# Two of four weight block sums of an MLP's first product: from VectorE to accumulating DMAs

## The chip, the cores and the metric

One core of one Trainium2 chip. The metric is the device time of one execution in microseconds (us); the runs shown are three, and their median is taken.

## The reference

One layer of an encoder on x of 512 tokens by 2048 features, all in float32: `h = x + conformer_conv(rms_norm(x))`, then `h = h + mlp(rms_norm(h))`, then a last RMS norm. Only the MLP matters here:

```python
def sq_relu_mlp(h, w_up, w_down):          # w_up [2048, 8192], w_down [8192, 2048]
    return jnp.square(jax.nn.relu(h @ w_up)) @ w_down
```

## The kernel before

**Matmuls.** A float32 product is made of float32r products: each operand is split into a high part (a cast) and a low part (what the cast left), and a product is three matmuls, high by high, high by low and low by high (`mm3`, lines 199 to 202). Weights are the stationary operand, 128 by 128; activations stream as 512 or 256 columns.

**Pieces.** All weights are fetched as a list of pieces of 512 KB (`pieces`, `fetch`, line 128), in the order in which TensorE (PE) uses them. A piece lands in a `wr` buffer by a DMA on SyncE's queue (SP), ScalarE (ACT) casts it into `wh` (the high part), VectorE (DVE) subtracts it into `wl` (the low part). `wr`, `wh` and `wl` have 3 buffers each. `prep(n)` (line 188) emits the fetches two pieces further than the splits.

**The first product (up).** It is computed with 7 block products in place of 8 (a scheme of Strassen and Winograd over 2 by 2 blocks). 32 units of 256 columns of `w_up`, four pieces to a unit. An up piece holds four blocks for two values of k (`wupb`, `BLOCKS` at line 105). Three block products use blocks 1 to 3 as they are (`OF_RAW`, line 825), four use sums of blocks (`OF_SUM`). `split_blocks` (line 169) makes both for a piece: ACT casts blocks 1 to 3 (line 178), DVE adds block 0 to blocks 1 and 2 (line 179: sums 0 and 1), then adds block 2 to sum 0 (line 182: sum 2) and block 3 to sum 2 (line 183: sum 3), takes the low part of the blocks (line 184); ACT casts the four sums (line 185) and DVE takes their low part (line 186). The sums lie in the tile `ws`, one buffer. A piece needs two `wh` and two `wl` buffers, one for the blocks and one for the sums, out of the three of each. On PE (function `up`, line 902) a piece is 18 matmuls with the blocks and then 24 with the sums, all of 256 columns.

**The second product (down).** Pieces of `wdn` of 256 rows by 512 columns; 24 matmuls of 512 columns each (`group`, line 785). Its sums are added to `h` by DVE (line 964).

**Order.** `jobs` (line 116) lists the work: up of units 0, 1 and 2, down of units 0 and 1, up of 3 and 4, down of 2 and 3, and so on, up of 29, 30 and 31, down of the last four. So up pieces come in runs: one of 12, then 13 of 8, then one of 12, with 16 down pieces between two of them. The order on PE is that of the program; on the other engines and the queues a scheduler orders the instructions of this part of the program, and each engine then keeps its order. The waits for buffers come from the tile framework.

**After a unit.** The block products are combined on DVE (lines 935 to 938, tile `c`, tag `W`), one operand having been copied by ACT into `q1` (line 934); relu and the RMS scale `r2` (line 940), the square (ACT, line 943) and the split into `z` (lines 950 and 951) follow. `r2` is made once: the column sums of `Q2` (tag `Q2`) are taken in unit 0 (`ffn_sum`, line 892), a power is taken on GpSimd (POOL, line 248, `rr_ffn`), and `ffn_scale` (line 897) writes `r2`. The tag `Q2` is used again at the end, for `Q3`.

Of the kernel before, what the change touches and what calls it, by code (L numbers as in the profile page):

```python
# [8 lines left out]
F32 = mybir.dt.float32  # L9
F32R = mybir.dt.float32r  # L10
AF = mybir.ActivationFunctionType
ALU = mybir.AluOpType
PSUM = bass.MemoryType.PSUM

P = 128
T = 512
# [11 lines left out]
HT = T // 2  # L28
EDGE = HT + 16

WBUFS = 3


POOL_TAPS = [5, 5, 6, 5] * 3 + [6, 5, 9]
# [15 lines left out]
N_UNITS = DFF // UNIT  # L50
# [4 lines left out]
def conformer_layer(ctx: ExitStack, tc: tile.TileContext, xT, vecs, wdw, w1, w2, wupb, wdn, outT):  # L55
    nc = tc.nc

    const = ctx.enter_context(tc.tile_pool(name="const", bufs=1))
    acts = ctx.enter_context(tc.tile_pool(name="acts", bufs=1))
    wpool = ctx.enter_context(tc.tile_pool(name="wpool", bufs=WBUFS))  # L60
    pp = ctx.enter_context(tc.tile_pool(name="pp", bufs=1, space=PSUM))
# [25 lines left out]
    def col(base, k):  # L87
        return vec[:, base + k : base + k + 1]


    pieces = []
# [10 lines left out]
        for k in range(0, NK, 2):  # L102
            wide(w2, k * P, g * 512)

    BLOCKS = [P, 2, 4, P]

    def up_pieces(u):
        for p in range(4):
            pieces.append((wupb[u, p], BLOCKS))

    def down_pieces(units):
        for g in range(4):
# [9 lines left out]
    for kind, what in jobs:  # L122
        (up_pieces if kind == "up" else down_pieces)(what)

    raws, prepped = {}, {}
    state = {"raw": 0, "prep": 0}

    def fetch(upto):
        while state["raw"] < min(upto, len(pieces)):
            i = state["raw"]  # L130
            src, shape = pieces[i]
            r = wtile(i, "wr", F32)
            if i < n_p1:
                for s in range(2):
                    nc.sync.dma_start(out=r[:, s], in_=src[:, s])
            elif shape is BLOCKS:
                nc.sync.dma_start(out=r.rearrange("p a b c -> p (a b c)"), in_=src)
            else:
                nc.sync.dma_start(out=r, in_=src)
            raws[i] = r  # L140
            state["raw"] += 1

    def home(i, tag):

        if i == n_p1 and tag != "wr":
            return ph1, tag, 1
        if (i < n_p1 and i % 4 == 3) or i == n_p1 + 4:
            return ph1, tag + "4", 1
        return wpool, tag, WBUFS

    def wtile(i, tag, dtype, shape=None):
        pool, tag, bufs = home(i, tag)
        return pool.tile(shape or pieces[i][1], dtype, tag=tag, name=f"{tag}{i}", bufs=bufs)
# [15 lines left out]
    def split_blocks(i):  # L169

        r = raws.pop(i)
        s = wpool.tile(BLOCKS, F32, tag="ws", name=f"ws{i}", bufs=1)
        hr, hs = (wpool.tile([P, 2, n, P], F32R, tag="wh", name=f"wh{i}_{n}", bufs=WBUFS) for n in (3, 4))
        lr, ls = (wpool.tile([P, 2, n, P], F32R, tag="wl", name=f"wl{i}_{n}", bufs=WBUFS) for n in (3, 4))
        prepped[i] = (hr, lr), (hs, ls)
        nc.scalar.copy(out=hr, in_=r[:, :, 1:4])  # L178
        nc.vector.tensor_tensor(
            out=s[:, :, 0:2], in0=r[:, :, 1:3], in1=r[:, :, 0:1].to_broadcast([P, 2, 2, P]), op=ALU.add  # L180
        )
        nc.vector.tensor_add(out=s[:, :, 2], in0=s[:, :, 0], in1=r[:, :, 2])
        nc.vector.tensor_add(out=s[:, :, 3], in0=s[:, :, 2], in1=r[:, :, 3])  # L183
        nc.vector.tensor_tensor(out=lr, in0=r[:, :, 1:4], in1=hr.bitcast(F32), op=ALU.subtract)
        nc.scalar.copy(out=hs, in_=s)  # L185
        nc.vector.tensor_tensor(out=ls, in0=s, in1=hs.bitcast(F32), op=ALU.subtract)  # L186

    def prep(upto):
        fetch(upto + 2)
        while state["prep"] < min(upto, len(pieces)):  # L190
            i = state["prep"]
            state["prep"] += 1
            if pieces[i][1] is BLOCKS:
                split_blocks(i)
# [4 lines left out]
    def mm3(out, wh, wl, xh, xl, start, stop, **kw):  # L199
        nc.tensor.matmul(out, lhsT=wh, rhs=xh, start=start, stop=False, **kw)  # L200
        nc.tensor.matmul(out, lhsT=wh, rhs=xl, start=False, stop=False, **kw)  # L201
        nc.tensor.matmul(out, lhsT=wl, rhs=xh, start=False, stop=stop, **kw)  # L202
# [3 lines left out]
    def bank(tag, name):  # L206
        return pp.tile([P, T], F32, tag=tag, name=name, bufs=banks_of[tag])
# [13 lines left out]
    def spread(dg, out, start=True):  # L221

        nc.tensor.matmul(
            out, lhsT=ones, rhs=dg.rearrange("p a b -> p (a b)"), start=start, stop=True, skip_group_check=True
        )
        return out
# [100 lines left out]
    with tc.manual_schedule(engines=ordered):  # L327
        added = 0
        for k in range(NK):
            ah[k], al[k] = split_scaled(k, x_of(k), col(C_GMIX, k))  # L330
            i, kk = divmod(k, 4)
            if i == 0 or kk % 2 == 0:
# [4 lines left out]
                    out=lo[:, :, part], in0=r, in1=hi[:, :, part].bitcast(F32), op=ALU.subtract  # L337
# [40 lines left out]
    box = {}  # L378
# [163 lines left out]
    for j in range(NK - 1):  # L542
# [16 lines left out]
        if j == NK - 3:  # L559
            box["dgw"] = ph1.tile([P, PE_TAPS, P], F32, tag="xn", name="dgw", bufs=1)  # L560
            for i in range(PE_TAPS):
                c = CW - 1 - i
# [5 lines left out]
    halves = (slice(0, HT), slice(HT, T))  # L568
    banks_a = pw1(last, 0, EDGE, more=True)
    fetch(n_p1 + 5)  # L570
    state["prep"] = n_p1 + 5
    split_hi(n_p1)
# [270 lines left out]
    def place(kt, b):  # L843
        o = pair_operand(kt)
        nc.scalar.copy(out=o[:, :, 0], in_=b[:, 0:7])
        nc.vector.tensor_tensor(out=o[:, :, 1], in0=b[:, 0:7], in1=o[:, :, 0].bitcast(F32), op=ALU.subtract)
        assert len(T4_OF) == kt
        T4_OF.append(o)

    hT = []  # L850
    Q2 = None
    for g in range(4):
# [7 lines left out]
        if g == 0:  # L860
            ph2 = ctx.enter_context(tc.tile_pool(name="ph2", bufs=2, reuse_waits="tile"))
            for i in range(4):
                t = ph2.tile([P, 4, T], F32, tag=f"h{i}", name=f"h{i}", bufs=1)
                nc.sync.dma_start(out=t, in_=xT[i * 4 * P : (i + 1) * 4 * P].rearrange("(k p) t -> p k t", p=P))
                hT.append(t)
            Q2 = ph2.tile([P, T], F32, tag="Q2", name="Q2", bufs=1)
        for m in range(4):
            k = 4 * g + m
            h = hT[g][:, m, :]
            nc.vector.scalar_tensor_tensor(  # L870
                out=h, in0=banks[m], scalar=col(C_BPW2, k), in1=h, op0=ALU.add, op1=ALU.add
            )
            if m % 2 == 0:
# [3 lines left out]
                out=blocks[:, at : at + 2].rearrange("p a b -> p (a b)"), in_=h, func=AF.Copy, scale=col(C_GFFN, k)  # L877
# [7 lines left out]
            if m % 2:  # L885
                form(k // 2, blocks)
                blocks_of[k // 2] = blocks
                if k // 2 < 3 or g == 3:
                    place(k // 2, blocks)
    r2 = const.tile([P, T], F32, name="r2")  # L890

    def ffn_sum():
        b = bank("x", "cs_ffn")
        colsum(b, 0, [Q2], 0, 4, True, True)
        box["dg"] = rms_scale(b, "ffn", ph2)

    def ffn_scale():
        nc.scalar.copy(out=r2, in_=spread(box["dg"], bank("x", "sp_ffn")))

    z_of = {}  # L900

    def up(u):

        n = ng["n"]
        ng["n"] += 1
        banks = [bank("mm" if n % 2 == 0 else "xxxy"[m], f"u{u}_{m}") for m in range(4)]
        i0 = pi["i"]
        pi["i"] += 4
        for p in range(4):
            prep(i0 + p + 2)  # L910
            for (wh, wl), of in zip(prepped.pop(i0 + p), (OF_RAW, OF_SUM)):
                for kk in range(2):
                    kt = 2 * p + kk
                    for b, (x, q, half) in enumerate(of):
                        out = banks[q][:, half * HT : half * HT + HT]
                        xh, xl = T4_OF[kt][:, x, 0], T4_OF[kt][:, x, 1]
                        first = kt == 0 and (of is OF_RAW or (q, half) == (2, 1))
                        mm3(out, wh[:, kk, b], wl[:, kk, b], xh, xl, first, kt == 7, skip_group_check=True)
                if u == 0 and p == 2 and of is OF_RAW:
                    ffn_sum()  # L920
        if u == 0:
            ffn_scale()

        def two(b):
            return b.rearrange("p (a t) -> p a t", a=2)


        c = ph2.tile([P, 6, HT], F32, tag="W", name=f"c{u}", bufs=1)
        q1 = ph2.tile([P, HT], F32, tag="q1", name=f"q1_{u}", bufs=1)

        def bc(a):
            return a[:, None, :].to_broadcast([P, 2, HT])

        nc.scalar.copy(out=q1, in_=banks[0][:, 0:HT])
        nc.vector.tensor_tensor(out=c[:, 2:6:2], in0=two(banks[1]), in1=bc(q1), op=ALU.add)
        nc.vector.tensor_tensor(out=c[:, 3:6:2], in0=two(banks[2]), in1=bc(c[:, 4]), op=ALU.add)
        nc.vector.tensor_tensor(out=c[:, 0:2], in0=two(banks[3]), in1=bc(c[:, 5]), op=ALU.subtract)
        nc.vector.tensor_sub(out=c[:, 3], in0=c[:, 3], in1=banks[3][:, HT:T])
        t = c[:, 0:4].rearrange("p (m a) t -> p m (a t)", m=2)
        nc.vector.scalar_tensor_tensor(  # L940
            out=t, in0=t, scalar=0.0, in1=r2[:, None, :].to_broadcast([P, 2, T]), op0=ALU.max, op1=ALU.mult
        )
        nc.scalar.activation(out=t, in_=t, func=AF.Square)
        if u == N_UNITS - 1:

            zh, zl = slots[0][:, 0:2], slots[0][:, 2:4]
        else:
            z = ph2.tile([P, 2, 2, T], F32R, tag="z", name=f"z{u}", bufs=3)
            zh, zl = z[:, 0], z[:, 1]
        nc.scalar.copy(out=zh, in_=t)  # L950
        nc.vector.tensor_sub(out=zl, in0=t, in1=zh.bitcast(F32))
        z_of[u] = [(zh[:, m], zl[:, m]) for m in range(2)]
# [21 lines left out]
    for g in range(3):  # L974
        banks = group(kc, zh, zl)
        for m in range(4):
            k = 4 * g + m
# [124 lines left out]
```

## Time and profile before

| | |
|---|---|
| median of 3 runs | 1964.34 us (1962.2 to 1964.91) |
| the profiled execution | 1961.89 us |
| its span, first to last instruction | 1959.8 us |
| busy share of the span | PE 98%, DVE 72%, ACT 38%, POOL 20% |
| mean granted clock of PE | 0.994 of full speed |

The rows of a profile say how long each engine was busy, what an engine waited for before it started an instruction (its releaser), and when each instruction started. "PE" is the matmuls; "PEld" the weight loads, which overlap them; a "q" behind an engine's name is its instruction queue, which issues DMAs. Matmuls are pipelined, so the time between two starts, not the duration of one, says how fast PE goes.

### The profile page before, as it was taken

The page shows a single profiled execution, that of the slowest core. Times are in us where ns is not written, and L with a number is a line of the kernel's source. Part 1 is how long each engine was busy: PE and PEld are TensorE (multiplying, and loading weights), DVE is VectorE, ACT ScalarE, POOL GpSimd, SP SyncE. Part 2 cuts the span into 40 slices and gives each one's busy share as a digit, 9 for nine tenths or more (in the row PEclk, how much of TensorE's full clock was granted, in tenths as well). Part 3 has the DMA queues.
Part 4 walks back from the last instruction along what each step waited for, and adds up shares of the span by engine and source line. Part 5 has one row for each costly group of instructions (what it writes and reads, how often), then busy time and mean ns, then how long its engine had stood idle before and what let it go on. Part 6 is the DMA issues. An engine that isn't in the chain of part 4 may idle for free.

```text
span 1959.8 us, 27630 instructions
## 1 busy us (share of the span) xinstructions
PE 1916.5 (98%) x11192; PEld 1697.3 (87%) x11192; DVE 1408.2 (72%) x1918; ACT 735.6 (38%) x903; POOL 386.5 (20%) x266
## 2 busy tenths in 40 slices
PE   8899999989999999999999999999999999999997
PEld 5688888878888898989989899898989989898987
DVE  7999999985468676767667676776767667675844
ACT  5533444553344332423324242332423333242443
POOL 6778899851111000000000000000000000000000
PEclk9999999999999999999999999999999999999999
DMA  7233333125322323333233332323323233333333
GB/s 221 76 97 97 97 97 98 55 72 172 98 86 80 108 87 108 108 91 114 86 112 94 96 112 92 109 87 108 108 86 117 82 113 90 105 108 88 111 99 101
DMA packets 138782, 199.23 MB, mean 102 GB/s; under 512 B 7328, under 2 KB 77216, under 8 KB 138656
## 3 DMA queue, kind: packets, MB, share of 16 engines
q1 hardware_dynamic: 138512, 197.42, 32.9%
q8 instruction: 87, 1.43, 0.3%
q14 instruction: 39, 0.32, 0.1%
q10 hardware_dynamic: 144, 0.07, 0.0%
HBM read 193.27 MB, written 4.19 MB: 101 GB/s over the span
## 4 chain that ended last, share of the span: by engine, by line
issue 69%; PE 24%; DVE 4%; DMA 1%; ACT 1%; SPq 0%; POOL 0%; POOLq 0%; DVEq 0%
PE g L201 3%; PE g L202 3%; PE g L200 3%; PE pa L202 3%; PE pa L201 3%; PE pg L200 3%; PE pg L202 3%; PE pa L200 3%; PE pg L201 3%; DVE slot L295 1%; DMA wr<-w 1%; DVE acc L432 0%; DVE slot L647 0%; DVE wl L167 0%; DMA x<-xT 0%
## 5 line engine op out<-in xcount | busy, mean ns | idle before, releaser
L162 ACT CAST wh<-wr 128x1024 fp32r<-128x1024 f32 x219 | 229.5, 1049 | 470.7 <-PE g L201 315.1
L200 PE MATMUL g<-z,wh 128*128 128x512 f32 (+1 forms) x1016 | 390.6, 384 | 0.0
L201 PE MATMUL g<-z,wh 128*128 128x512 f32 (+1 forms) x1016 | 390.3, 384 | 0.0
L202 PE MATMUL g<-z,wl 128*128 128x512 f32 (+1 forms) x1016 | 390.1, 384 | 0.0
L167 DVE TENSOR_TENSOR wl<-wr,wh 128x1024 fp32r<-128x1024 f32 x159 | 200.5, 1262 | 213.3 <-ACT wh L162 213.1
L202 PE MATMUL u<-slot,wl 128*128 128x256 f32 x1120 | 319.6, 285 | 5.6 <-DVE wl L186 3.7
L200 PE MATMUL u<-slot,wh 128*128 128x256 f32 x1120 | 317.6, 284 | 0.1
L201 PE MATMUL u<-slot,wh 128*128 128x256 f32 x1120 | 317.4, 283 | 0.0
L186 DVE TENSOR_TENSOR wl<-ws,wh 128x1024 fp32r<-128x1024 f32 x128 | 156.8, 1225 | 187.9 <-ACT wh L185 187.0
L248 POOL TENSOR_TENSOR rr_fin<-ms_fin,mhalf 128x2 f32<-128x2 f32 x2 | 1.4, 696 | 1341.3 <-DVE ms_fin L246 1341.3
L185 ACT CAST wh<-ws 128x1024 fp32r<-128x1024 f32 x128 | 134.1, 1048 | 294.7 <-DVE ws L183 138.3
L432 DVE SCALAR_TENSOR_TENSOR acc<-u,wd,acc 128x512 f32<-128x512 f32 (+1 forms) x362 | 237.4, 729 | 0.2
L202 PEld LDWEIGHTS u<-slot,wl 128*128 128x128 f32 x1120 | 215.3, 192 | 9.7 <-DVE wl L186 7.8
L202 PEld LDWEIGHTS g<-z,wl 128*128 128x128 f32 x1016 | 190.9, 188 | 37.8
L200 PEld LDWEIGHTS g<-z,wh 128*128 128x128 f32 x1016 | 190.9, 188 | 37.6
L201 PEld LDWEIGHTS g<-z,wh 128*128 128x128 f32 x1016 | 190.9, 188 | 37.1
L200 PEld LDWEIGHTS u<-slot,wh 128*128 128x128 f32 x1120 | 215.4, 192 | 0.4 <-ACT wh L185 0.3
L201 PEld LDWEIGHTS u<-slot,wh 128*128 128x128 f32 x1120 | 215.4, 192 | 0.0
L202 PE MATMUL u<-T,wl 128*128 128x256 f32 x672 | 190.7, 284 | 1.9 <-DVE wl L186 1.8
L200 PE MATMUL u<-T,wh 128*128 128x256 f32 x672 | 190.7, 284 | 1.0 <-ACT wh L185 1.0
L201 PE MATMUL u<-T,wh 128*128 128x256 f32 x672 | 190.1, 283 | 0.0
L178 ACT CAST wh<-wr 128x768 fp32r<-128x768 f32 x128 | 106.8, 834 | 214.2 <-PE g L201 122.7
(207 smaller groups left out, 3484.0 us busy)
## 6 DMA issues: line engine op xcount, KB each, us to landing
wr<-wupb SPq DMA_DIRECT2D x128, 512.0 KB, 3.6
wr<-wdn SPq DMA_DIRECT2D x128, 512.0 KB, 3.7
wr<-w SPq DMA_DIRECT2D x120, 256.0 KB, 3.3
wr<-w SPq DMA_DIRECT2D x32, 512.0 KB, 3.7
h<-xT SPq DMA_DIRECT2D x4, 1024.0 KB, 10.8
outT<-h SPq DMA_DIRECT2D x14, 256.0 KB, 2.9
x<-xT SPq DMA_DIRECT2D x6, 512.0 KB, 6.0
wr<-w SPq DMA_DIRECT2D x16, 128.0 KB, 5.3
```

The source lines that it names most:

```text
L162: nc.scalar.copy(out=prepped[i][0], in_=r)
L167: eng.tensor_tensor(out=lo, in0=r, in1=hi.bitcast(F32), op=ALU.subtract)
L178: nc.scalar.copy(out=hr, in_=r[:, :, 1:4])
L185: nc.scalar.copy(out=hs, in_=s)
L186: nc.vector.tensor_tensor(out=ls, in0=s, in1=hs.bitcast(F32), op=ALU.subtract)
L200: nc.tensor.matmul(out, lhsT=wh, rhs=xh, start=start, stop=False, **kw)
L201: nc.tensor.matmul(out, lhsT=wh, rhs=xl, start=False, stop=False, **kw)
L202: nc.tensor.matmul(out, lhsT=wl, rhs=xh, start=False, stop=stop, **kw)
L248: nc.gpsimd.tensor_tensor(out=r, in0=ms, in1=mhalf[:, 0:n], op=ALU.pow)
L295: nc.vector.scalar_tensor_tensor(out=lo, in0=src, scalar=g, in1=hi.bitcast(F32), op0=ALU.mult, op1=ALU.subtract)
L432: nc.vector.scalar_tensor_tensor(out=acc if c < end - 1 else vt, in0=u[:, c : c + n], scalar=wd[:, j, c : c + 1], in1=src, op0=ALU.mult, o ...
```

## The change

The weights for up are laid out by the host with the block index ahead of k, so that the tiles are `[P, block, 2, P]`. An up piece's `wr` tile holds blocks 1 to 3 only (384 KB in place of 512 KB). `ws` has two buffers, and is allocated and partly filled when the piece is fetched: one more DMA on SP writes blocks 1 and 2 into its places 0 and 1 (256 KB), and a DMA issued by POOL adds block 0, read from DRAM once for each of the two places, onto both (256 KB). The addition on line 179 is left out. To make room, `r2` moves into the buffer of `Q2`, and `q1` into place 0 of `c`.

```diff
--- before.py
+++ after.py
@@ -29,6 +29,7 @@
 EDGE = HT + 16
 
 WBUFS = 3
+WSBUFS = 2
 
 
 POOL_TAPS = [5, 5, 6, 5] * 3 + [6, 5, 9]
@@ -102,11 +103,11 @@
         for k in range(0, NK, 2):
             wide(w2, k * P, g * 512)
 
-    BLOCKS = [P, 2, 4, P]
+    BLOCKS = [P, 4, 2, P]
 
     def up_pieces(u):
         for p in range(4):
-            pieces.append((wupb[u, p], BLOCKS))
+            pieces.append((wupb[u, p].rearrange("p (b k c) -> p b k c", b=4, k=2), BLOCKS))
 
     def down_pieces(units):
         for g in range(4):
@@ -122,19 +123,30 @@
     for kind, what in jobs:
         (up_pieces if kind == "up" else down_pieces)(what)
 
-    raws, prepped = {}, {}
+    raws, prepped, sums_of = {}, {}, {}
     state = {"raw": 0, "prep": 0}
 
     def fetch(upto):
         while state["raw"] < min(upto, len(pieces)):
             i = state["raw"]
             src, shape = pieces[i]
-            r = wtile(i, "wr", F32)
+            if shape is BLOCKS:
+                r = wtile(i, "wr", F32, [P, 3, 2, P])
+            else:
+                r = wtile(i, "wr", F32)
             if i < n_p1:
                 for s in range(2):
                     nc.sync.dma_start(out=r[:, s], in_=src[:, s])
             elif shape is BLOCKS:
-                nc.sync.dma_start(out=r.rearrange("p a b c -> p (a b c)"), in_=src)
+                nc.sync.dma_start(out=r, in_=src[:, 1:4])
+
+                s = sums_of[i] = wpool.tile([P, 4, 2, P], F32, tag="ws", name=f"ws{i}", bufs=WSBUFS)
+                nc.sync.dma_start(out=s[:, 0:2], in_=src[:, 1:3])
+                nc.gpsimd.dma_start(
+                    out=s[:, 0:2].rearrange("p b k c -> p b (k c)"),
+                    in_=src[:, 0:1].rearrange("p b k c -> p b (k c)").to_broadcast([P, 2, 2 * P]),
+                    accum_op=ALU.add,
+                )
             else:
                 nc.sync.dma_start(out=r, in_=src)
             raws[i] = r
@@ -171,17 +183,14 @@
 
 
         r = raws.pop(i)
-        s = wpool.tile(BLOCKS, F32, tag="ws", name=f"ws{i}", bufs=1)
-        hr, hs = (wpool.tile([P, 2, n, P], F32R, tag="wh", name=f"wh{i}_{n}", bufs=WBUFS) for n in (3, 4))
-        lr, ls = (wpool.tile([P, 2, n, P], F32R, tag="wl", name=f"wl{i}_{n}", bufs=WBUFS) for n in (3, 4))
+        s = sums_of.pop(i)
+        hr, hs = (wpool.tile([P, n, 2, P], F32R, tag="wh", name=f"wh{i}_{n}", bufs=WBUFS) for n in (3, 4))
+        lr, ls = (wpool.tile([P, n, 2, P], F32R, tag="wl", name=f"wl{i}_{n}", bufs=WBUFS) for n in (3, 4))
         prepped[i] = (hr, lr), (hs, ls)
-        nc.scalar.copy(out=hr, in_=r[:, :, 1:4])
-        nc.vector.tensor_tensor(
-            out=s[:, :, 0:2], in0=r[:, :, 1:3], in1=r[:, :, 0:1].to_broadcast([P, 2, 2, P]), op=ALU.add
-        )
-        nc.vector.tensor_add(out=s[:, :, 2], in0=s[:, :, 0], in1=r[:, :, 2])
-        nc.vector.tensor_add(out=s[:, :, 3], in0=s[:, :, 2], in1=r[:, :, 3])
-        nc.vector.tensor_tensor(out=lr, in0=r[:, :, 1:4], in1=hr.bitcast(F32), op=ALU.subtract)
+        nc.scalar.copy(out=hr, in_=r)
+        nc.vector.tensor_add(out=s[:, 2], in0=s[:, 0], in1=r[:, 1])
+        nc.vector.tensor_add(out=s[:, 3], in0=s[:, 2], in1=r[:, 2])
+        nc.vector.tensor_tensor(out=lr, in0=r, in1=hr.bitcast(F32), op=ALU.subtract)
         nc.scalar.copy(out=hs, in_=s)
         nc.vector.tensor_tensor(out=ls, in0=s, in1=hs.bitcast(F32), op=ALU.subtract)
 
@@ -887,14 +896,13 @@
                 blocks_of[k // 2] = blocks
                 if k // 2 < 3 or g == 3:
                     place(k // 2, blocks)
-    r2 = const.tile([P, T], F32, name="r2")
-
     def ffn_sum():
         b = bank("x", "cs_ffn")
         colsum(b, 0, [Q2], 0, 4, True, True)
         box["dg"] = rms_scale(b, "ffn", ph2)
 
     def ffn_scale():
+        r2 = box["r2"] = ph2.tile([P, T], F32, tag="Q2", name="r2", bufs=1)
         nc.scalar.copy(out=r2, in_=spread(box["dg"], bank("x", "sp_ffn")))
 
     z_of = {}
@@ -915,7 +923,7 @@
                         out = banks[q][:, half * HT : half * HT + HT]
                         xh, xl = T4_OF[kt][:, x, 0], T4_OF[kt][:, x, 1]
                         first = kt == 0 and (of is OF_RAW or (q, half) == (2, 1))
-                        mm3(out, wh[:, kk, b], wl[:, kk, b], xh, xl, first, kt == 7, skip_group_check=True)
+                        mm3(out, wh[:, b, kk], wl[:, b, kk], xh, xl, first, kt == 7, skip_group_check=True)
                 if u == 0 and p == 2 and of is OF_RAW:
                     ffn_sum()
         if u == 0:
@@ -926,7 +934,8 @@
 
 
         c = ph2.tile([P, 6, HT], F32, tag="W", name=f"c{u}", bufs=1)
-        q1 = ph2.tile([P, HT], F32, tag="q1", name=f"q1_{u}", bufs=1)
+
+        q1 = c[:, 0]
 
         def bc(a):
             return a[:, None, :].to_broadcast([P, 2, HT])
@@ -938,7 +947,7 @@
         nc.vector.tensor_sub(out=c[:, 3], in0=c[:, 3], in1=banks[3][:, HT:T])
         t = c[:, 0:4].rearrange("p (m a) t -> p m (a t)", m=2)
         nc.vector.scalar_tensor_tensor(
-            out=t, in0=t, scalar=0.0, in1=r2[:, None, :].to_broadcast([P, 2, T]), op0=ALU.max, op1=ALU.mult
+            out=t, in0=t, scalar=0.0, in1=box["r2"][:, None, :].to_broadcast([P, 2, T]), op0=ALU.max, op1=ALU.mult
         )
         nc.scalar.activation(out=t, in_=t, func=AF.Square)
         if u == N_UNITS - 1:
@@ -1064,8 +1073,8 @@
     def blocks(w):
 
         w = w.reshape(4, 2, 2, P, N_UNITS, 2, P)
-        w = np.stack([w[:, :, 1, :, :, 0], w[:, :, 0, :, :, 0], w[:, :, 1, :, :, 1], w[:, :, 0, :, :, 1]], axis=4)
-        return np.ascontiguousarray(w.transpose(3, 0, 2, 1, 4, 5)).reshape(N_UNITS, 4, P, 8 * P)
+        w = np.stack([w[:, :, 1, :, :, 0], w[:, :, 0, :, :, 0], w[:, :, 1, :, :, 1], w[:, :, 0, :, :, 1]], axis=3)
+        return np.ascontiguousarray(w.transpose(4, 0, 2, 3, 1, 5)).reshape(N_UNITS, 4, P, 8 * P)
 
     arrays = {
         "xT": np.ascontiguousarray(a["x"][0].T),
```

## Rows read from the trace of the kernel before

**Rows 1.** The page's first part: busy time, share of the span, instructions.

```profile
span 1959.8 us, 27630 instructions
PE 1916.5 (98%) x11192; PEld 1697.3 (87%) x11192; DVE 1408.2 (72%) x1918; ACT 735.6 (38%) x903; POOL 386.5 (20%) x266
```

**Rows 2.** Windows: stretch, length, busy time (instructions) by engine, PE clock, DMA share, GB/s.

```profile
600.00:640.00 40.00, 37.20 (x294) 35.49 (x294) 32.73 (x47) 15.30 (x20) 1.93 (x1) 1.00 0.30 91
...
800.00:900.00 100.00, 99.99 (x662) 92.28 (x662) 70.91 (x96) 35.60 (x39) 0.00 (x0) 1.00 0.31 96
1300.00:1400.00 100.00, 99.98 (x662) 92.27 (x662) 70.28 (x95) 34.57 (x38) 0.00 (x0) 1.00 0.32 99
...
1800.00:1850.00 50.00, 48.20 (x393) 47.18 (x392) 39.81 (x57) 21.00 (x24) 0.00 (x0) 1.00 0.33 95
```

**Rows 3.** Waits of PE in the up pieces: us in total, times, longest.

```profile
PE u L202 <- DVE wl L186: 5.5, 9, 0.9
...
PE u L202 <- DVE wl L184: 1.7, 1, 1.7
...
PE u L200 <- ACT wh L185: 1.0, 2, 0.5
```

**Rows 4.** Timeline of PE around 1204 us: start, duration, what.

```profile
1200.05 0.39 PE L200 MATMUL g<-z,wh 128*128 128x512 f32 x1
1200.27 0.39 PE L201 MATMUL g<-z,wh 128*128 128x512 f32 x1
...
1204.12 0.28 PE L200 MATMUL u<-T,wh 128*128 128x256 f32 x1
1204.24 0.28 PE L201 MATMUL u<-T,wh 128*128 128x256 f32 x1
...
1209.16 0.28 PE L200 MATMUL u<-T,wh 128*128 128x256 f32 x1
```

**Rows 5.** Timeline of ACT in that run of eight up pieces.

```profile
1206.40 1.05 ACT L185 CAST wh<-ws 128x1024 fp32r<-128x1024 f32 x1 [1.46 <-PE u L201]
...
1222.37 1.05 ACT L185 CAST wh<-ws 128x1024 fp32r<-128x1024 f32 x1 [0.76 <-DVE ws L183]
...
1241.96 0.37 ACT L934 COPY q<-u 128x256 f32<-128x256 f32 x1 [0.31 <-PE u L202]
```

**Rows 6.** Timeline of DVE in that run of eight up pieces.

```profile
1207.48 1.23 DVE L186 TENSOR_TENSOR wl<-ws,wh 128x1024 fp32r<-128x1024 f32 x1 [1.51 <-ACT wh L185]
...
1220.51 0.96 DVE L184 TENSOR_TENSOR wl<-wr,wh 128x768 fp32r<-128x768 f32 x1 [0.88 <-ACT wh L178]
1221.38 0.42 DVE L182 TENSOR_TENSOR ws<-ws,wr 128x256 f32<-128x256 f32 x1
...
1223.45 1.22 DVE L186 TENSOR_TENSOR wl<-ws,wh 128x1024 fp32r<-128x1024 f32 x1 [1.19 <-ACT wh L185]
...
1233.21 1.22 DVE L951 TENSOR_TENSOR z<-c,z 128x1024 fp32r<-128x1024 f32 x1
```

**Rows 7.** Groups by line: count, busy us, mean ns of one, idle before, releaser.

```profile
L179 DVE TENSOR_TENSOR ws<-wr 128x512 f32<-128x512 f32 x128 | 88.1, 688 | 7.1 <-DMA wr<-wupb 5.1
...
L185 ACT CAST wh<-ws 128x1024 fp32r<-128x1024 f32 x128 | 134.1, 1048 | 294.7 <-DVE ws L183 138.3
...
L178 ACT CAST wh<-wr 128x768 fp32r<-128x768 f32 x128 | 106.8, 834 | 214.2 <-PE g L201 122.7
```

**Rows 8.** DMA issues: count, KB each, median us from issue to landing.

```profile
wr<-wupb SPq DMA_DIRECT2D x128, 512.0 KB, 3.6
...
wr<-w SPq DMA_DIRECT2D x120, 256.0 KB, 3.3
...
outT<-h SPq DMA_DIRECT2D x14, 256.0 KB, 2.9
...
outT<-h SPq DMA_DIRECT2D x4, 128.0 KB, 1.8
```

**Rows 9.** The DMA queue of SP: packets, MB, share of 16 engines.

```profile
q1 hardware_dynamic: 138512, 197.42, 32.9%
```

**Rows 10.** Tile wupb: the issuing of its DMAs on SP's queue, duration min/median/max in ns.

```profile
L137 SPq DMA_DIRECT2D wr<-wupb x128: 327/328/341, 558.2 to 1833.3; - x128
```

## The prediction

> **What bounds the kernel now.** I read the page's busy shares first: PE is busy for 98% of the span, and DVE, which the change relieves, for 72% [rows 1]. A share over the whole span proves little, so I cut it: in stretches inside the MLP PE is busy for 99.98 of 100 us, and DVE for 70 of them [rows 2]. The reader is to see that nothing keeps PE waiting there. The gaps that exist lie in the first and the last run of twelve up pieces: 2.8 us in 40 and 1.8 us in 50 [rows 2]. The waits name their causes: PE waited 5.5 us for the low part of the sums, 1.7 for that of the blocks and 1.0 for the cast of the sums, 8.2 us together [rows 3]. That is all that faster preparation of up weights could win; the 88.1 us of additions on line 179 [rows 7] lie beside a busy PE.
>
> Then I took PE's beat from the timeline: a matmul of 256 columns starts every 0.12 us, a piece of 42 every 5.04 (1204.12 to 1209.16), and one of 512 columns every 0.22 to 0.23 [rows 4]. So an up piece allows 5.04 us for everything its weights need. I call S(k) the start of piece k in the run of eight that begins at 1204.12. PE needs the first low part of the sums 18 matmuls and two more later: at S(k) + 2.16 + 0.24 = S(k) + 2.40.
>
> Last I looked at how early the sums are ready. Piece 1 has its low part at 1207.48 + 1.23 = 1208.71 [rows 6], against a need at 1209.16 + 2.40 = 1211.56: 2.85 us to spare. It can't be much earlier, since ACT began the cast at 1206.40, when PE released the `wh` buffer [rows 5].
>
> **What the change costs, part by part.**
>
> *Removed:* 128 additions of 0.69 us on DVE [rows 7]. Cover: PE. Worth 0 where PE doesn't wait, at most the 8.2 us above.
>
> *Layout:* the blocks' cast now reads one straight stretch. Its 768 elements took 834 ns and the sums' 1024, already straight, 1048 [rows 7]: 0.81 us for 768 by proportion where 0.83 was measured. Nothing to win. `q1` in place 0 of `c` must wait for the last reader of the previous `c`, which started at 1233.21 [rows 6] and ran 1.22; `q1` is written at 1241.96 [rows 5]: 7.5 us to spare, so 0. `r2` and `Q3` take over `Q2`'s buffer a group or more after its last reader: 0. The power for the RMS scale shares POOL's queue with the new DMAs in unit 0 and could stand behind one that waits: once, 0 to about 3 us; I take 0.
>
> *SP's queue:* a DMA keeps it 0.33 us [rows 10], two per up piece 0.66 of 5.04. More important, the new DMA of piece k waits until line 186 has freed `ws` of piece k-2, and the blocks of piece k+1 are queued behind it. For piece 4 that is 1208.71. Landing takes 3.6 [rows 8], the cast 0.83 [rows 7] and line 184 0.96 [rows 6]: ready by about 1214.1, where PE starts piece 4 at 1204.12 + 4 x 5.04 = 1224.28. Cost 0, and if PE stalls, the need moves too.
>
> *Bytes:* a piece moves 384 + 256 + 256 = 896 KB in place of 512. The SP queue's packets fill 32.9% of the engines [rows 9], 0.31 to 0.33 in the MLP [rows 2]; times 1.75 that is 0.58 in the up runs. Not a bound, but the landings may lengthen.
>
> *The new chain.* This carries the sum. Sums 0 and 1 no longer come from a 0.69 us instruction on data that landed long ago, but from two DMAs in a row, and the first can't start before the buffer is free. With two buffers a loop closes every two pieces: `ws` freed by line 186 of piece k-2; copy of 256 KB; accumulation, x; lines 182, 183, cast, line 186 of piece k. The copy: 3.3 us (256 KB on this queue; bounds 2.9 for the output's 256 KB, 3.6 for 512 KB [rows 8]). The last part can be read off: line 182 started at 1221.38, the cast at 1222.37, line 186 at 1223.45 for 1.22 [rows 5, 6], so 3.29. The loop is 6.59 + x, against 10.08 that PE takes for two pieces.
>
> Some spare time is used up first. From 1208.71 (piece 1) to the need of piece 7, 1204.12 + 7 x 5.04 + 2.40 = 1241.80, there are 33.09 us for three loops. A run of eight thus stalls PE by 3 (6.59 + x) - 33.09 = 3x - 13.3, from x = 4.44 on. A run of twelve has 53.25 us for five loops: 5x - 20.3, from 4.06 on. The chain of even pieces starts earlier and is looser. After each run 16 down pieces let it recover, so the stalls add up: 13 runs of eight, 2 of twelve.
>
> *The price x.* No row shows an accumulating DMA. Below it is a plain transfer of these bytes, 2.9 [rows 8]; above, two whole transfers in turn, the destination read and then written, 6.6. I take 5.1: the plain 3.3 on this queue and, since the old value must be fetched before the new one can be written, the shortest trip of the page, 1.8 for 128 KB [rows 8]. The Trainium skill, "DMA: Bandwidth & Descriptors", section "Rules for kernel authors", says that an accumulate reads its destination and writes it later; no row here shows it. The same page, section "Anatomy of one DMA — SWDGE (gpsimd) path", fits a DMA from GpSimd as 2.0 us plus the bytes at 436 GB/s, an estimate of 2.6 here, by which there would be no stall at all.
>
> *Behind the waiting addition:* line 182 is now the instruction that waits for the DMA, and DVE is in order. If line 184 of the same piece stands behind it, the blocks' low part is needed earlier: 0.42 twice and 0.96 after the DMA for a need at S(k) + 0.24, 0.7 us stricter than the sums' 3.29 for S(k) + 2.40. In the row line 184 stands ahead (1220.51 against 1221.38 [rows 6]), but the scheduler may choose anew: 0 to 0.7 in each of 15 late runs, 0 to 10.6 us. I take 5.
>
> *The sum* with x = 5.1: 13 x 1.98 + 2 x 5.2 = 36, plus 5 for the order: 41 us. The removed additions win nothing, since the sums then come from the late chain. The profiled execution took 1961.9 us (span 1959.8 and 2.1 around it), 2.45 below the median: 2003 against it, 2005 against the median. Bounds: x = 2.9 gives 0; x = 6.6 gives 13 x 6.5 + 2 x 12.7 = 110, with 10.6 for the order 121, so 2085. A copy of 2.9 or 3.6 shifts x by -0.4 or +0.3: at 5.1 the stalls are 15 or 51 in place of 36.
>
> **The rivals.**
>
> *A, no change: the accumulation is hidden.* The place is the two-buffer loop, the price x, and the deciding point 4.1 to 4.4. For it: plain transfers of these bytes take 2.9 to 3.3, POOL is idle in the MLP and the DMA engines are two thirds free [rows 2, 8, 9]. Against: it needs the second trip to cost under about 1.1, less than any landing of the page. Time: about 1964, not slower. The fit cited above speaks for this one.
>
> *B, faster: as A, and PE's 8.2 us of waits go*, because DVE has 0.69 us less per piece in the runs of twelve where they occur. Time 1956. Against: those are the runs with the least room, x below 4.06, and part of the waits is for ACT.
>
> *C, much slower: x of 9 or more*, an accumulation slower than two transfers in turn, or one that queues behind the blocks' transfers. At 9 the runs lose 13.7 and 24.7: 13 x 13.7 + 2 x 24.7 = 227, time about 2190. For it: no row excludes it. Against: 256 KB need little of engines 0.58 busy.
>
> **How the numbers follow.** Forecast (x between 4.4 and 7, slower) 0.53; A 0.24; B 0.08; C 0.14; 0.01 for other things. The time is the forecast's, 2005. A measurement of this kernel can tell about 0.2%, 3.9 us, from no change. Faster by that needs B: 0.08. Same: A, with a few cases at the foot of the forecast, 0.25. Slower: the rest and C, 0.67. The range takes in A down to B's edge, 1957, and above x = 7: 13 x 7.7 + 2 x 14.7 = 129 and 10 for the order, 2105. It leaves out C and half of B. The forecast's own range is 1970 to 2105.
>
> **What would show it.** Right: PE's wait for line 186 grows from 5.5 us to some 35, in pieces late in each run, while down stretches stay full; line 182 waits for a DMA; the POOL queue's accumulation lands about 5 us after its issue, and SP waits for line 186. If landing is under 4 and PE's waits don't grow, the price was wrong and A or B holds. If it lands in time and PE stalls all the same, the order on DVE, or POOL's queue, is what I have mis-sized.

## The result, and the profile after

The changed kernel takes 2104.5 us (median of 4 runs, 2102.7 to 2108.2) against 1964.6 us before: ratio 1.072, 95% interval 1.070 to 1.074. I had forecast 2005 us, in a range up to 2105: the direction was right, the size was not, a loss of 140 us where I had 41.

The page of after, busy shares, the new queue and the DMA issues, beside [rows 1, 8, 9]:

```profile
span 2102.1 us, 28226 instructions
PE 1960.2 (93%) x11192; PEld 1727.7 (82%) x11192; DVE 1323.6 (63%) x1790; ACT 733.5 (35%) x903; POOL 546.2 (26%) x394
...
q0 software_dynamic: 34816, 33.56, 10.7%
...
ws<-wupb SPq DMA_DIRECT2D x128, 256.0 KB, 3.2
ws<-wupb POOLq DMA_DIRECT2D x128, 256.0 KB, 4.8
```

DVE lost its 85 us of additions, as meant. The two prices of the new chain are near the ones I took: 3.2 for the copy (I had 3.3) and 4.8 for the accumulation (5.1). By the fit of the Trainium skill that I had cited ("DMA: Bandwidth & Descriptors", section "Anatomy of one DMA — SWDGE (gpsimd) path"), an estimate of 2.6, the loss would have been none; the measurement decides.

The waits of PE and of the weight loads in the up pieces of after, beside [rows 3]:

```profile
PE u L211 <- DVE wl L193: 75.6, 44, 3.6
PE u L211 <- DVE wl L195: 24.2, 32, 5.5
...
PEld u L211 <- DVE wl L193: 84.9, 46, 3.8
PEld u L211 <- DVE wl L195: 30.7, 32, 5.7
PEld u L209 <- ACT wh L194: 4.5, 7, 0.9
```

Line 193 is the low part of the blocks, 195 that of the sums (184 and 186 before). PE waits for the blocks more than for the sums: DVE stands at the addition that waits for the DMA, with the blocks' subtraction queued behind it.

From the first matmul of the first up piece to the last of the down pieces (tiles u and g, first and last start) the MLP took 1499.3 us (585.8 to 2085.1) where it took 1360.1 before (583.0 to 1943.1). So the loss, 139 us, is all there, and inside it all in the up runs: each stretch of down pieces between two of them takes 43.7 us before and after, while a run of eight takes 49.4 us from its first matmul to its last (mean of 13) where it took 40.5, and the two runs of twelve take 11.1 and 12.7 more.

**One run of eight.** It begins on PE at 1270.98:

```profile
1270.98 0.28 PE L209 MATMUL u<-T,wh 128*128 128x256 f32 x1
```

The timelines of SP, POOL and DVE of after show the copy and the accumulation of its odd pieces (the accumulation at 1286.29 is an even piece's), then lines 191 (the first to need it) and 195. The first line 191 shown is that of piece 2, the first line 195 that of piece 1:

```profile
1277.94 0.33 SPq L144 DMA_DIRECT2D ws<-wupb  x1
...
1289.43 0.33 SPq L144 DMA_DIRECT2D ws<-wupb  x1
...
1302.63 0.33 SPq L144 DMA_DIRECT2D ws<-wupb  x1
...
1316.81 0.33 SPq L144 DMA_DIRECT2D ws<-wupb  x1
```

```profile
1281.32 1.21 POOL L145 DMA_DIRECT2D ws<-wupb  x1 [8.97 <-DMA ws<-wupb]
1286.29 1.20 POOL L145 DMA_DIRECT2D ws<-wupb  x1 [3.77 <-issue]
1293.29 1.23 POOL L145 DMA_DIRECT2D ws<-wupb  x1 [5.79 <-DMA ws<-wupb]
...
1308.10 1.23 POOL L145 DMA_DIRECT2D ws<-wupb  x1 [7.99 <-DMA ws<-wupb]
```

```profile
1275.89 0.43 DVE L191 TENSOR_TENSOR ws<-ws,wr 128x256 f32<-128x256 f32 x1 [3.10 <-DMA ws<-wupb]
...
1276.70 1.22 DVE L195 TENSOR_TENSOR wl<-ws,wh 128x1024 fp32r<-128x1024 f32 x1
...
1286.06 0.43 DVE L191 TENSOR_TENSOR ws<-ws,wr 128x256 f32<-128x256 f32 x1 [5.45 <-DMA ws<-wupb]
...
1288.17 1.23 DVE L195 TENSOR_TENSOR wl<-ws,wh 128x1024 fp32r<-128x1024 f32 x1 [0.36 <-ACT wh L194]
...
1297.58 0.43 DVE L191 TENSOR_TENSOR ws<-ws,wr 128x256 f32<-128x256 f32 x1 [2.76 <-DMA ws<-wupb]
...
1301.38 1.22 DVE L195 TENSOR_TENSOR wl<-ws,wh 128x1024 fp32r<-128x1024 f32 x1
...
1312.76 0.42 DVE L191 TENSOR_TENSOR ws<-ws,wr 128x256 f32<-128x256 f32 x1 [4.45 <-DMA ws<-wupb]
```

Each copy on SP starts when the low part of the piece two before is done, so the distance of the odd pieces' copies is my loop. The first turn, 1277.94 to 1289.43, is 11.49 us: 3.38 to POOL's start, 4.74 to line 191, 3.34 to the end of line 195. I had 11.69. The second is 13.20: line 195 comes 3.80 after line 191, not 2.11, with the combination of the unit between them on DVE. The third is 14.18: 5.47 from the copy to POOL, with loads of down pieces issued just before and after it, and 4.02 from line 191 to the end of 195. Together 38.9 us, where I had 35.1. The run is no extreme one: in the 13 runs of eight the three turns take 38.6 to 41.1 us together, 39.4 in the mean.

The chain also starts later than I took it. Line 195 of piece 1 ends at 1277.92, 6.9 us after the run's start; in before it was 4.6 (1208.71 for a start at 1204.12). On DVE it stands behind line 191 of piece 2, which waits until 1275.89 for an accumulation of its own. In the 13 runs it is 6.2 to 7.8, so some 30.7 us are left for the three turns and not the 33.1 of my sum.

**What a stall costs beyond itself.** PE's timeline in after, at the last piece of that run:

```profile
1311.21 0.28 PE L210 MATMUL u<-slot,wh 128*128 128x256 f32 x1
1314.11 0.39 PE L211 MATMUL u<-slot,wl 128*128 128x256 f32 x1 [2.62 <-DVE wl L193]
...
1316.08 0.41 PE L210 MATMUL u<-slot,wh 128*128 128x256 f32 x1
1316.29 0.41 PE L211 MATMUL u<-slot,wl 128*128 128x256 f32 x1
...
1319.21 0.28 PE L210 MATMUL u<-slot,wh 128*128 128x256 f32 x1
1319.33 0.28 PE L211 MATMUL u<-slot,wl 128*128 128x256 f32 x1
```

and windows there (length, PE, PEld, DVE, ACT, POOL, clock, DMA share, GB/s):

```profile
1308.00:1313.00 5.00, 3.13 (x24) 2.93 (x24) 0.55 (x2) 0.00 (x0) 1.23 (x1) 1.00 0.68 167
...
1316.00:1318.00 2.00, 2.00 (x11) 2.00 (x10) 2.00 (x3) 1.68 (x3) 0.00 (x0) 0.50 1.01 269
```

After a wait of 2.62 us and more than a microsecond of full speed, PE runs for some 3 us with a beat of 0.21 in place of 0.12: the granted clock is 0.50, the lower of the two levels, 1.2 of 2.4 GHz. Over the whole run the mean clock is 0.977 of 2102.1 us against 0.994 of 1959.8: 48 us of full speed not granted against 12.

Windows over the MLP, before and after, give PE's own account of the loss:

```profile
583.00:1943.10 1360.10, 1351.51 (x8537) 1228.80 (x8537) 927.37 (x1231) 466.07 (x521) 11.90 (x8) 1.00 0.32 99
```

```profile
585.80:2085.10 1499.30, 1391.96 (x8536) 1257.04 (x8535) 844.31 (x1105) 463.99 (x521) 168.45 (x134) 0.98 0.47 123
```

PE is idle for 107.3 us where it was for 8.6, and busy for 40.5 more with the same work: 139 together. Of the idle time, 102.9 us are the waits in the up pieces (8.2 before). Another 4.5 are one wait in unit 0, for the RMS scale:

```profile
PE cs_ffn L243 <- POOL Q L893: 4.5, 1, 4.5
```

### The profile page after: what moved, and what is told of

It reads as the page before. It is cut to its first block, busy times and chain, and to the rows that moved or that the text cites. A ratio compares the mean times of both kernels' runs of the same rounds, so it can differ in the third digit from the quotient of the medians.

```text
span 2102.1 us, 28226 instructions
## 1 busy us (share of the span) xinstructions
PE 1960.2 (93%) x11192; PEld 1727.7 (82%) x11192; DVE 1323.6 (63%) x1790; ACT 733.5 (35%) x903; POOL 546.2 (26%) x394
## 4 chain that ended last, share of the span: by engine, by line
PE 62%; DMA 21%; DVE 9%; issue 4%; ACT 2%; POOL 1%; SPq 0%; POOLq 0%; DVEq 0%; ACTq 0%
DMA ws<-wupb 20%; PE g L210 13%; PE g L209 13%; PE g L211 13%; PE u L211 3%; DVE wl L195 3%; PE u L210 3%; PE u L209 3%; PE pa L210 2%; PE pa L211 2%; PE pg L210 2%; PE pg L209 2%; PE pg L211 2%; PE pa L209 2%; ACT wh L194 2%
## 5 line engine op out<-in xcount | busy, mean ns | idle before, releaser
L145 POOL DMA_DIRECT2D ws<-wupb x128 | 156.0, 1219 | 1272.4 <-DVE h L973 573.9
L211 PE MATMUL u<-slot,wl 128*128 128x256 f32 x1120 | 330.7, 295 | 51.7 <-DVE wl L193 42.9
L209 PE MATMUL u<-slot,wh 128*128 128x256 f32 x1120 | 325.5, 291 | 1.4 <-ACT wh L194 1.4
L210 PE MATMUL u<-slot,wh 128*128 128x256 f32 x1120 | 325.0, 290 | 0.0
L211 PEld LDWEIGHTS u<-slot,wl 128*128 128x128 f32 x1120 | 223.1, 199 | 62.0 <-DVE wl L193 49.2
L191 DVE TENSOR_TENSOR ws<-ws,wr 128x256 f32<-128x256 f32 x128 | 54.5, 425 | 325.5 <-DMA ws<-wupb 271.6
L211 PE MATMUL u<-T,wl 128*128 128x256 f32 x672 | 197.2, 293 | 48.1 <-DVE wl L193 32.7
L209 PEld LDWEIGHTS u<-slot,wh 128*128 128x128 f32 x1120 | 223.4, 199 | 2.2 <-ACT wh L194 2.2
L210 PEld LDWEIGHTS u<-slot,wh 128*128 128x128 f32 x1120 | 223.0, 199 | 0.0
L209 PE MATMUL u<-T,wh 128*128 128x256 f32 x672 | 194.4, 289 | 1.7 <-ACT wh L194 1.7
L210 PE MATMUL u<-T,wh 128*128 128x256 f32 x672 | 193.5, 288 | 0.0
```

What stands on the lines that cost most here:

```text
L145: nc.gpsimd.dma_start(out=s[:, 0:2].rearrange("p b k c -> p b (k c)"), in_=src[:, 0:1].rearrange("p b k c -> p b (k c)").to_broadcast([P, ...
L191: nc.vector.tensor_add(out=s[:, 2], in0=s[:, 0], in1=r[:, 1])
```

## The experiments

**e1: the addition back on DVE, the rest of the layout kept.**

```diff
-                nc.sync.dma_start(out=r, in_=src[:, 1:4])
...
+                nc.sync.dma_start(out=r, in_=src)
...
+        nc.vector.tensor_tensor(
+            out=s[:, 0:2], in0=r[:, 1:3], in1=r[:, 0:1].to_broadcast([P, 2, 2, P]), op=ALU.add
+        )
```

> The changed kernel with the addition of block 0 back on VectorE, whole pieces of 512 KB and one sums buffer; the new weight layout and the places of r2 and q1 stay. If only the DMA chain costs time: 1961 to 1967 us, no change to the kernel before. If the layout or the moved tiles cost part of the 140 us: clearly above 1970.

1964.1 us, ratio 0.9996 (0.9987 to 1.0006). Layout, `q1` and `r2` cost nothing; the loss belongs to the DMAs and to what waits for them.

**e2: no addition of block 0 at all.**

```diff
-                nc.gpsimd.dma_start(
...
-                    accum_op=ALU.add,
-                )
```

> Leaves out the addition of block 0 to sums 0 and 1 altogether; the 256 KB copy on SyncE's queue and the two buffers stay. Loop theory (two buffers, copy and accumulation in a row): the loop falls from 11.5 us or more to 3.2 + 3.3 = 6.5 against 10.08 that TensorE takes for two pieces, so no stall: 1956 to 1966 us, which is also the most that relieving VectorE could ever win. Rival, the bytes on the DMA engines: 256 of the 384 added KB are gone, of the 140 us some 45 to 90 stay: 2010 to 2050 us.

1948.7 us, ratio 0.991 (0.989 to 0.993). No stall, as the loop theory says, but below my 1956: relieving DVE, with the second buffer, is worth 16 us, twice what I had called the most. The weight loads show most of it. Their waits before, which I had not put into my rows,

```profile
PEld u L202 <- DVE wl L186: 10.7, 24, 1.1
PEld u L202 <- DVE wl L184: 1.9, 1, 1.9
PEld u L200 <- ACT wh L185: 1.7, 3, 0.7
```

come to 14.3 us, where the waits of PE gave 8.2 [rows 3]; in e2 3.6 us of them are left. A matmul's row lasts 0.28 us at a beat of 0.12 [rows 4], so a gap of up to 0.16 us leaves PE "busy" and counts as no wait.

**e3: the same DMA without the addition** (block 0 written over the copy).

```diff
-                    accum_op=ALU.add,
```

> Leaves out the addition: the DMA from GpSimd's queue writes block 0 over the two places where it was added to them, same bytes, same queue, same waits. Loop theory: only its own time from start to landing counts, 4.8 us accumulating; every us less of it is worth 3 us in a run of eight and 5 in a run of twelve, 49 us in all. If a plain one lands in 3.8 us: 2040 to 2065 us; if it lands in 4.6 or more, adding costs next to nothing by itself and the time stays at 2085 to 2105. Rival, the bytes: about 2104 whatever the landing.

2021.7 us, ratio 1.029 (1.026 to 1.032). A plain one lands in 4.0 us and keeps POOL 0.72 us where the accumulating one takes 4.8 and 1.21:

```profile
ws<-wupb POOLq DMA_DIRECT2D x128, 256.0 KB, 4.0
```

With bytes, queue and waits as in after, 83 us are gone, so the bytes aren't the cause of these; of the 57 that stay e3 can't tell, and e8 does. The time is below the 2040 to 2065 us that I expected, and 83 is twice the 39 us that 0.8 us of price are worth at 49 per microsecond. Every engine has its instructions in the order of after, so all of the 83 us come from the addition, but not from its price in the three turns alone: the chain starts 1.3 us earlier in a run of eight (5.5 against 6.9 after the run's start), and POOL's late starts (e5) are gone too.

**e4: sums 0 and 1 in three buffers of their own.** The same memory and the same DMAs.

```diff
-WSBUFS = 2
+WSBUFS = 3
...
+        t = wpool.tile([P, 2, 2, P], F32, tag="wt", name=f"wt{i}", bufs=1)
+        nc.vector.tensor_add(out=t[:, 0], in0=s[:, 0], in1=r[:, 1])
+        nc.vector.tensor_add(out=t[:, 1], in0=t[:, 0], in1=r[:, 2])
...
+        for h, part in ((0, s), (2, t)):
+            nc.scalar.copy(out=hs[:, h : h + 2], in_=part)
...
```

> Sums 0 and 1 in a tile of their own with three buffers, sums 2 and 3 in another with one, so the same memory and the same DMAs; the cast and the subtraction of the sums go in two halves. Loop theory: the loop of 11.5 to 14 us now closes every three pieces, 15.12 us, so the stalls go: 1960 to 1980 us. Rival, one accumulation at a time on GpSimd's queue (4.95 us apart when they follow one another, against 5.04 a piece): little room, 1975 to 2040 us. Rival, the bytes on the DMA engines: unchanged, 2090 to 2110 us.

1962.6 us, ratio 0.9987 (0.9978 to 0.9996). The stalls of the MLP are gone; it takes 1350.1 us, 10 less than before. But it begins at 594.7, 11.7 us late: the first buffers are free from the start, and the scheduler puts their DMAs among POOL's first instructions. After has two of them there, at 37 and 43 us; here a third, at 49.8, stands ahead of the power for the first RMS scale, and PE waits 9.0 us once for that scale.

**e5: more room for the descriptors of POOL's DMAs.** All engines' orders are those of after.

```diff
-dynamic_dma_scratch_size=1024
+dynamic_dma_scratch_size=1408
```

> The changed kernel, every engine's order the same, with 1408 bytes per partition in place of 1024 reserved for the descriptors of GpSimd's DMAs. In the profile of after GpSimd starts some accumulations late by up to 4 us though their copy has landed, just when the accumulation before has landed (idle put down to 'issue', 70 us, 20 times). If that room holds one accumulation and not two: these waits go, and the time falls to 2060 to 2095 us. If they have another cause: 2098 to 2110 us, and the waits stay.

2078.3 us, ratio 1.058 (1.056 to 1.060), 26 less than after. In after POOL's waits had this line, and e5 has none of it:

```profile
POOL ws L145 <- issue: 70.0, 20, 4.2
```

In the timeline of POOL above, the accumulation at 1286.29 is such a case: its copy was issued at 1280.63, and it starts just after the accumulation before has landed (line 191 at 1286.06). So with 1024 bytes one accumulation is in flight at a time: none of the 128 in after starts before the one ahead of it has landed, and in e5 31 do. The Trainium skill ("DMA: Bandwidth & Descriptors", section "SWDGE vs HWDGE vs iDMA") says that GpSimd writes its descriptors to rings in a reserved part of SBUF; the run agrees and shows what a small part costs.

**e6: DVE's order, the blocks' low part first.**

```diff
+        with tc.manual_schedule(engines={mybir.EngineType.DVE}):
+            nc.vector.tensor_tensor(out=lr, in0=r, in1=hr.bitcast(F32), op=ALU.subtract)
...
```

> The changed kernel with VectorE's order fixed within a piece: low part of the blocks first, then sums 2 and 3 (the instructions that wait for the accumulation). My forecast put 0.7 us per run on this order. If the chain of sums is what is late: TensorE's 75.6 us of waits for the low part of the blocks go over to the low part of the sums, win about 0.7 us per late run, 2085 to 2100 us. Rival, the order makes most of the loss: those waits go without return, 2020 to 2050 us.

2075.9 us, ratio 1.056 (1.052 to 1.060), 29 less than after, between the two expectations. The waits turn into these:

```profile
PE u L212 <- DVE wl L196: 40.0, 55, 1.7
PE u L210 <- ACT wh L195: 37.4, 39, 2.8
```

77 us for the sums in place of 100 for blocks and sums: the order makes the lateness worse and isn't its source.

**e7: copy and accumulation made for nobody beside e1.**

```diff
+                x = ph2.tile([P, 2, 2, P], F32, tag="wx", name=f"wx{i}", bufs=2)
+                nc.sync.dma_start(out=x, in_=src[:, 1:3])
+                nc.gpsimd.dma_start(
...
```

> The kernel of e1 (VectorE adds, whole pieces) that also makes the copy of 256 KB and the accumulating DMA for each up piece, into a tile of two buffers that nothing reads: 1024 KB a piece where the changed kernel moves 896. Loop theory: nobody waits for them, 1960 to 1970 us. Rival, the bytes or GpSimd's descriptors slow the loads or the engines: above 1985 us.

2302.7 us, ratio 1.172 (1.170 to 1.174), and no test of the bytes. Since nothing reads the tile, the scheduler put the 128 pairs ahead of their pieces (439 to 1168 us), and SP, in order, stood before the copies with the weight loads behind them:

```profile
SPq L143 <- DMA wx<-wupb: 625.5, 126, 7.1
```

It shows what a waiting DMA does to what is queued behind it, and says nothing on contention. e8 answers that.

**e8: e4 with the tile of sums 0 and 1 in the pool that opens after the convolution stage.**

```diff
-                s = sums_of[i] = wpool.tile([P, 2, 2, P], F32, tag="ws", name=f"ws{i}", bufs=WSBUFS)
+                s = sums_of[i] = ph2.tile([P, 2, 2, P], F32, tag="ws", name=f"ws{i}", bufs=WSBUFS)
```

> The kernel of e4 (three buffers) with the tile of sums 0 and 1 in the pool that opens at the end of the convolution stage, so that its first DMAs can't be put among GpSimd's instructions of the first 50 us, where in e4 TensorE waited 9 us more and the MLP began 11.7 us later. In e4 the MLP took 1349.8 us from its first matmul to its last, 10 less than before. If the two are independent: 1948 to 1956 us, faster than before. If the early stage was late for another reason: 1958 to 1965 us.

1946.9 us, ratio 0.992 (0.990 to 0.994): faster than both kernels, and just below the 1948 to 1956 that I expected. Its middle, 700 to 1800 us, and its DMA issues:

```profile
700.00:1800.00 1100.00, 1100.00 (x6949) 1002.62 (x6948) 703.60 (x999) 375.77 (x502) 127.97 (x106) 1.00 0.53 139
```

```profile
ws<-wupb SPq DMA_DIRECT2D x128, 256.0 KB, 3.6
ws<-wupb POOLq DMA_DIRECT2D x128, 256.0 KB, 5.0
```

The DMAs are those of after, they even land later, and PE is never without work. The MLP takes 1346.9 us (581.6 to 1928.5), 13.2 less than before; of the waits of the weight loads one of 2.8 us is left. So neither the price of the accumulation nor the bytes cost anything by themselves; they cost where the loop must close in two pieces. e8 changes two things against after, the third buffer and a tile that comes free earlier; e9 takes them apart.

**e9: e8 with two buffers.**

```diff
-WSBUFS = 3
+WSBUFS = 2
```

> The kernel of e8 with two buffers for sums 0 and 1 in place of three, nothing else. If only the third buffer counted: back to 2075 to 2105 us. By the loop it should be less: the buffer now holds sums 0 and 1 alone and comes free after the first half of the cast and of the subtraction, so the loop is 3.2 + 4.8 + some 1.6 = 9.6 us when nothing collides, just under 10.08, and up to 12 where the down pieces' loads or the combination of a unit collide: 1975 to 2040 us.

2039.4 us, ratio 1.040 (1.038 to 1.042): the third buffer alone is worth 92 us. That it isn't 2104 fits the shorter loop that comes with the smaller tile.

**e10: e8 with e5 and e6.**

> e8 with the order of e6 on VectorE and the descriptor room of e5. In e8 one wait of 2.6 us for the low part of the blocks is all that is left in the up pieces, so either helps by 0 to 3 us: 1942 to 1950 us. Rival, one accumulation at a time still limits e8: 1935 to 1941.

1951.8 us, ratio 0.9945 (0.993 to 0.996), no better than e8 and just above the 1942 to 1950 that I expected. With three buffers there is nothing left for either to cure.

**e11: after with e5 and e6.**

> The changed kernel with both e5's room and e6's order, two buffers of the whole tile. Each alone won 26 and 28 us. If they act on separate parts of a late run, they add: 2045 to 2060 us, and some 85 us of the loss stay with the loop of two buffers. If they cure the same waits: 2065 to 2078.

2071.8 us, ratio 1.056 (1.054 to 1.058). The two don't add: each shortens the same late chain, and some 107 us of loss stay with two buffers of the whole tile.

## Why the prediction was wrong in size

The mechanism (a loop over two buffers that doesn't close in time) and the direction were right, and so were the prices of the loop: copy 3.2 for 3.3, accumulation 4.8 for 5.1, a turn without collision 11.49 for 11.69, and the layout, `q1` and `r2` at nothing (e1). Rivals A, B and C fell: it was neither hidden nor slower than two transfers.

The step that failed is the sum, "13 x 1.98 + 2 x 5.2 = 36, plus 5 for the order", in two of its terms. First, it took the turn without collision for every turn of a run: 35.1 us for three, where the runs show 39.4. In the run shown the turns were 11.5, 13.2 and 14.2: the second carries a unit's combination on DVE, the third the loads of the down pieces. Both stood in the profile of before at those places: SP began to issue the down pieces' loads at 1229.01, and DVE took 4.09 us from line 182 to the end of line 186 in the piece with the combination, against the 3.29 that I read off the piece before it:

```profile
1227.27 0.42 DVE L182 TENSOR_TENSOR ws<-ws,wr 128x256 f32<-128x256 f32 x1
...
1230.14 1.22 DVE L186 TENSOR_TENSOR wl<-ws,wh 128x1024 fp32r<-128x1024 f32 x1
```

I had written that the landings may lengthen, and given it no number. Second, "From 1208.71 (piece 1)" took the start of the chain from before. The chain of even pieces that I called looser delays it: line 191 of piece 2 waits ahead of line 195 of piece 1 on DVE. That is 2.3 us a run in the mean. With the forecast's 1.98 and the turns' 4.4 it makes 8.6 of the 8.9 us by which a run of eight is longer. PE's waits were 6.5 us in the run shown (1.37, 1.66, 0.38, 0.42 and 2.62), 5.1 to 7.3 in all runs of eight, and 9.5 and 11.7 in the runs of twelve; the rest of the 8.9 lies in matmuls that took longer, at the slow clock above all.

Three other terms were missing or too small. They are parts of the same lateness, seen from other sides, and can't be added to it or to one another (e11). The clock: no step had one, and 36 us of full speed went there. One accumulation at a time: not in any step, 26 us by e5. The order on DVE: at most 10.6 by my bound, 29 by e6, which takes line 193 out from behind a late line 191. My sign of being right came true in part: the wait for the low part of the sums grew to 24.2 us, not 35, and that for the blocks, which I had not named, from 1.7 to 75.6.

The worth of the removed additions was misread as well: "at most the 8.2 us" came from the waits of PE; e2 shows 16 us and e8 13 in the MLP. And the RMS scale on POOL's queue, "0 to about 3 us; I take 0", cost PE a wait of 4.5 once; what held POOL there is not shown.

What stays open is how much the transfers slow one another. In the third turn SP issued the copy 0.03 us after the release. It took 4.8 us to land, against 2.7 in the first turn, and POOL started 0.7 us after that, as in the first. So neither SP's order nor POOL held it. The DMA engines were full as it began (DMA share 1.13):

```profile
1302.60:1304.90 2.30, 2.25 (x18) 2.25 (x19) 2.00 (x2) 1.10 (x2) 0.00 (x0) 1.00 1.13 319
```

From 1304.90 to POOL's start at 1308.10 their share was 0.34. Whether the copy was slow for their load or for its place behind the down piece's load on the same DMA queue, no run tells apart; e7 was to tell and did not.

## What to carry to other kernels

When an instruction on resident data is replaced by DMAs into a rotating buffer, time the whole loop from the buffer's release to its next release, with the worst neighbours that it meets, against the time that the consumer takes for as many pieces as there are buffers. Look also at what stands before each step of the loop on an engine that keeps its order: an instruction of the next piece that waits for a DMA holds up this one. Here two buffers of the whole tile lost 7%; three of half the tile, in the same memory, won 0.8%. Look for the slow clock after a stall of PE, and judge PE's slack by the waits of the weight loads too.

## What the runs showed that I had not expected

After a wait of 2.62 us PE did not slow at once: more than a microsecond at full beat, then some 3 us at granted clock 0.50. Other waits differ: after 1.78 us, ended at 834.0, the clock was 0.50 from 834.3 on, and after 2.49 us, ended at 757.1, it stayed at 1.00 for the next 5 us. An accumulating DMA of 256 KB from POOL cost only 0.8 us more to landing than a plain one (4.8 against 4.0), and 0.5 us more of POOL (1.21 against 0.72). With 1024 bytes per partition for descriptors POOL had one such accumulation in flight, with 1408 it no longer waited. And a tile that is free from the start lets the scheduler place its first DMA more than 500 us ahead of its use, on a queue where it delays others (e4).
